# Residual projections by 512-column weight row tiles in one ring of eight PSUM banks, with regrouped stage seams

## The chip, the cores and the metric

The kernel runs on one core of a Trainium2 chip. The metric is the device time of one execution in microseconds, as the median of several runs. A core has a matrix engine (TensorE, PE in the profile), three engines for elementwise work (VectorE or DVE, ScalarE or ACT, GpSimd or POOL) and SyncE (SP), which here issues nearly all DMA transfers. Each engine has its own instruction list, which it works through in order; an instruction that waits for a semaphore holds up everything behind it on its engine. Matmuls read SBUF and accumulate in PSUM, which has eight banks of 128 partitions by 512 fp32 values.

## What is computed

One layer of a trunk block over 1024 tokens of width 1024, in fp32: a token mixer (RWKV-7 and HGRN2 branches, merged by gates), cross-attention into 256 memory tokens with four heads, and a SwiGLU feed-forward part, each with an RMSNorm before and a residual add behind, then a last RMSNorm.

```python
u = rmsnorm(h, norm_mix_g[l])
cols = u @ w_in[l]
...
h = h + (gate_a * y_a + gate_b * y_b) @ w_out[l]

u = rmsnorm(h, norm_xa_g[l])
m = rmsnorm(mem, norm_mem_g[l])
q = (u @ xa_wq[l]).reshape(B, S, XA_HEADS, XA_HEAD)
k = (m @ xa_wk[l]).reshape(B, n_mem, XA_HEADS, XA_HEAD)
v = (m @ xa_wv[l]).reshape(B, n_mem, XA_HEADS, XA_HEAD)
...
h = h + o @ xa_wo[l]

u = rmsnorm(h, norm_ffn_g[l])
h = h + (jax.nn.silu(u @ ffn_w1[l]) * (u @ ffn_w3[l])) @ ffn_w2[l]
...
return rmsnorm(h, norm_final_g)
```

The two products whose tiling changes are those by `w_out` and by `xa_wo`, each 1024 by 1024, each followed by a residual add.

## The kernel before

**Precision.** Every large product is done with split operands: a tile is copied by ACT into a rounded high part (`split`, L281), and POOL or DVE subtracts that from the tile for the low part (L285). A product of two split operands is three matmuls (`mm3`, L299 to L301: high by high, low by high, high by low). So each weight tile costs a DMA load, an ACT copy, a subtraction on POOL or DVE, and three matmuls per use. `P` is 128 rows, `HALF` 512 columns, `KT` 8 tiles of the contracted dimension, `NHALF` 2.

**The order.** The code is written in program order, and a scheduler builds each engine's list from it; parts in a `high_priority` block are pulled forward. Generators that are stepped by `next` inside a loop (`beside`, `late`) put other work into that loop's order.

**The stages.** Up to about 1299 us the mixer runs. `attention_block` follows: keys and values from the memory tokens (`pk`, `pvv`; `load_w` loads 256-column weight groups as four tiles of two row blocks, L1668), then the first residual projection, by `w_out`, then per half of the tokens and per head the queries (`pq`), scores (`psc`), softmax, transposes (`ptp`) and outputs (`po`), then the second residual projection, by `xa_wo`, for one half of the tokens after the other.

**The residual projections** (`add_project`, tile `pw`) go by four column groups of 256. For a group the four weight tiles are loaded and split; then for each pair of tokens tiles (128 tokens each) all eight `k` are run into one PSUM tile, and DVE adds it to the residual (L1758). A matmul has 256 columns. Between the pairs `beside` is stepped. For `w_out` and the first half of `xa_wo` that is `w2_sums`, which forms sums of blocks of `ffn_w2` for the last phase (loads `y` at L1713, a DVE and a POOL sum at L1717 and L1718, a store to `wsum_d` at L1721): seven of its eleven steps under `w_out`, four under `xa_wo`. Under the second half of `xa_wo` it is `early_blocks`, which prepares the FFN's operand blocks of the first half of the tokens.

**PSUM** in this stage is three pools: two banks for transposes, three for projections, three for scores and outputs.

**The FFN** forms its products by a Strassen-like scheme: sums of operand blocks, seven products (`P1` to `P7`) for each pair of row blocks. The products that need only the first half of the tokens are run first for `AHEAD` = 2 groups (`early_products`); the blocks of the second half (`late_blocks`: L1976 to L1981, operands `hB`, `lB`, `fS`, `hS`, `lS`) are made in two lumps ahead of and behind them.

**The last phase** multiplies by `ffn_w2`: seven blocks of eleven items. An item is a hidden tile (`tl`, loaded at L2194, split into `th` by ACT at L2200 and `tl` by DVE at L2201) and a weight tile (`wraw` from `ffn_w2` or `wsum_d`, L2176; split into `wh` by ACT and `wl` by POOL), and twelve matmuls of 512 columns into four accumulators `acc`. Loads run 8 items ahead, splits 4 ahead. At a block's end the accumulators are added into `hres`. After the fifth block, the first half of the tokens is complete: each token tile is scaled (`finish`, L2139 and L2143, DVE) and stored (L2142 and L2146, SP) at once. Then the second half follows, and the program ends.

Of the kernel before, what the change touches and what calls it, by code (L numbers as in the profile page):

```python
# [2 lines left out]

# [6 lines left out]
F32 = mybir.dt.float32  # L10
# [173 lines left out]
def tile_trunk(ctx, tc, x, mem, norm_mix_g, w_in, rw_mu, rw_w0, rw_w2, rw_a0, rw_a2, rw_g2,  # L184
# [1456 lines left out]
    ssq = const.tile([P, 4, 4], F32, name="ssq")  # L1641
# [5 lines left out]
    def attention_block(xctx):  # L1647
# [14 lines left out]
        def load_w(src, col, lo_eng=None, queue=nc.sync):  # L1662

            s3 = src[0, :, col:col + W].rearrange("(k p) c -> p k c", p=P)
            w = []
            for k in range(0, KT, 2):
                raw = rp.tile([P, 2, W], F32, tag="wraw", name="wraw")
                queue.dma_start(out=raw, in_=s3[:, k:k + 2, :])  # L1668
                hi, lo = (wp.tile([P, 2, W], F32R, tag=n, name=n) for n in ("whi", "wlo"))
# [10 lines left out]
        with tc.high_priority(4000):  # L1680
            w0 = load_w(xa_wv, 0, queue=nc.scalar)
# [3 lines left out]
        for c in range(D // W):  # L1685
            if 2 * c >= KEYS:
                w = load_w(xa_wk, c * W)
                for t in range(2):
                    ps = pp.tile([P, HALF], F32, tag="proj", name="pk")
# [6 lines left out]
            w = load_w(xa_wv, c * W) if c else w0  # L1696
            ps = pp.tile([P, NMT, W], F32, tag="proj", name="pvv")
# [9 lines left out]
        def w2_sums(fs, places):  # L1707
# [16 lines left out]
            for place in places:  # L1724
                if place:
                    y = place()
                    f = next(fs)
                    load(f, y)
                    loaded.append((f, y))
                    if len(loaded) < 3:  # L1730
                        yield
                        continue
                if loaded:
                    sums(*loaded.pop(0))
                yield
            for l in loaded:
                sums(*l)
                yield

        def add_project(a, w, src, halves, ss=None, beside=iter(()), every=False):  # L1740


            hs = []
            for c in range(D // W):
                ww = load_w(w, c * W)
                for i2 in range(2 * halves.start, 2 * halves.stop):
                    if c == 0:
                        hs += load_tokens(hp, src, 2 * i2, 2)
                    ps = pp.tile([P, 2, W], F32, tag="proj", name="pw")
                    for n in range(2):  # L1750
                        i = 2 * i2 + n
                        ah, al = a[i // 4]
                        ts_ = slice((i % 4) * P, (i % 4 + 1) * P)
                        for k in range(KT):
                            mm3(ps[:, n, :], ah[:, k, ts_], al[:, k, ts_], *ww[k], k == 0, k == KT - 1)
                    for n in range(2):
                        o = hs[2 * i2 + n - 4 * halves.start][:, c * W:(c + 1) * W]
                        nc.vector.tensor_tensor(o, ps[:, n, :], o, op=ALU.add)  # L1758
                        if ss is not None:
                            junk = sp.tile([P, D], mybir.dt.bfloat16, tag="junk", name="junkw", bufs=1)[:, 0:W]  # L1760
                            nc.scalar.activation(junk, o, AF.Square, accum_out=ss[:, 2 * i2 + n - 4 * halves.start, c:c + 1])
                    if every or c > 1 or c == 1 and i2 % 2:
                        next(beside, None)
            return hs

        def early_blocks(hs, hi, lo):

            sums = act2.tile([P, KT, HALF], F32, tag="ah", name="sums")
            for k in range(HK):
                pts = []  # L1770
                for kk in (k, k + HK):
                    pts.append(pt_.tile([P, HALF], F32, tag="tr", name="pt"))
                    for i in range(4):
                        nc.tensor.transpose(pts[-1][:, i * P:(i + 1) * P], hs[i][:, kk * P:(kk + 1) * P], ident)
                b12, s1 = sums[:, k, :], sums[:, k + HK, :]
# [8 lines left out]
                if k % 2:  # L1784
                    yield


        yT = []
        for h in range(NHALF):
            a = act((act0, act1)[h])  # L1790
# [4 lines left out]
            yT.append(a)  # L1795
# [4 lines left out]
        def in_act2(tag, n):  # L1800
# [6 lines left out]
        hs = add_project(yT, w_out, x[0], range(NHALF), every=True, beside=w2_sums(  # L1807
            w2f, [None, None] + [in_act2(tag, n) for tag in ("ah", "al", "ah") for n in range(2)] + [in_act2("al", 0)]))
        xaT = []
        for h in range(NHALF):  # L1810
            for i in range(4):
                nc.sync.dma_start(out=h1d[(4 * h + i) * P:(4 * h + i + 1) * P, :], in_=hs[4 * h + i])
            normalize(hs[4 * h:4 * h + 4], sp)
            a = act((act0, act1)[h])
            transpose_split(hs[4 * h:4 * h + 4], "xa", *a, slice(0, HALF), pt_)
            xaT.append(a)
# [4 lines left out]
        def weights(h, hd):  # L1821
# [4 lines left out]
            for t in range(2):  # L1826
                ps = pp.tile([P, HALF], F32, tag="proj", name="pq")
# [8 lines left out]
            for i2 in range(2):  # L1836
                ps = px.tile([P, 2, NM], F32, tag="x", name="psc")
# [17 lines left out]
        def attended(o, hd, p):  # L1855
            pTh = hp.tile([P, NMT, HALF], F32R, tag="h", name="pTh")
            pTl = hp.tile([P, NMT, HALF], F32R, tag="h", name="pTl")
            for mt in range(NMT):
                pt = pt_.tile([P, HALF], F32, tag="tr", name="ptp")
# [396 lines left out]
```

## Time and profile before

| | us |
|---|---|
| median of 3 runs (range) | 2383.24 (2382.25 to 2384.34) |
| the profiled execution | 2381.83 |
| its span | 2380.1 |
| mean granted TensorE clock | 0.990 of full |
| first and last `pw` matmul | 1357.6, 1709 |
| last phase, from and to | 2147, 2372 |

A row of the timeline gives a start and a duration in us, the engine, the line, and the operation as output <- inputs with its shape. In brackets stands how long the engine was idle before it, and what it waited for. A group row gives the number of instructions, their busy time and mean ns, and then the idle time before them. Matmuls are pipelined, so that the distance between their starts tells their cost, not their duration. The rows themselves stand in the prediction, beside the steps that use them.

### The profile page before, as it was taken

How to read it: one execution, taken by the hardware profiler on the slowest of the kernel's cores; microseconds unless marked ns; L12 is line 12 of the kernel's file. 1: busy time of each engine (PE TensorE's matmuls, PEld its weight loads, DVE VectorE, ACT ScalarE, POOL GpSimd, SP SyncE). 2: the span in 40 equal slices, each digit the busy share in tenths (PEclk: the TensorE clock that was granted, in tenths of full speed). 3: DMA queues.
4: the chain of work that ended last, by engine and by line, in shares of the span. 5: the costliest groups of instructions: out<-in, count | busy, mean ns of one | idle time of the engine just before them, and what ended most of it. 6: DMA issues, size and time to landing. Idle time of an engine off the chain costs nothing. (4 is left out here: it accounts for less than half of the span.)

```text
span 2380.1 us, 48890 instructions
## 1 busy us (share of the span) xinstructions
PE 2311.5 (97%) x19126; PEld 1913.0 (80%) x19126; DVE 1515.4 (64%) x2397; ACT 1136.1 (48%) x2271; POOL 1235.6 (52%) x1257
## 2 busy tenths in 40 slices
PE   7999999999999999999999999999989999999997
PEld 5777777778887878888887998889968888888876
DVE  5887874667777667766755545444577565566454
ACT  6545454545566646565564515442452333334432
POOL 3554545555566555675564741113465655556544
PEclk9999999999999999999999999999999999999999
DMA  5444445333334344434244893128643433348552
GB/s 176 116 126 119 124 119 166 70 95 85 103 102 121 78 130 107 114 90 115 64 150 142 272 339 128 63 70 305 201 136 100 128 100 100 111 151 319 181 173 93
DMA packets 397668, 325.97 MB, mean 137 GB/s; under 512 B 107467, under 2 KB 330813, under 8 KB 396029
## 3 DMA queue, kind: packets, MB, share of 16 engines
q1 hardware_dynamic: 395005, 317.08, 43.9%
q0 software_dynamic: 1344, 4.72, 0.5%
q8 instruction: 151, 2.47, 0.4%
q10 hardware_dynamic: 1088, 1.05, 0.1%
q14 instruction: 80, 0.66, 0.1%
HBM read 226.03 MB, written 96.21 MB: 135 GB/s over the span
## 5 line engine op out<-in xcount | busy, mean ns | idle before, releaser
L102 PE MATMUL pproj<-uh,whi 128*128 128x512 f32 x768 | 320.3, 417 | 0.9 <-DVE q L102 0.7
L102 PE MATMUL pproj<-uh,wlo 128*128 128x512 f32 x768 | 301.0, 392 | 3.2 <-POOL wlo L102 2.3
L102 PE MATMUL pproj<-ul,whi 128*128 128x512 f32 x768 | 301.4, 392 | 0.0
L285 POOL TENSOR_TENSOR wl<-wraw,wh 128x512 fp32r<-128x512 f32 x143 | 202.0, 1427 | 153.3 <-ACT wh L281 139.9
L285 POOL TENSOR_TENSOR wlo<-wraw,whi 128x512 fp32r<-128x512 f32 (+1 forms) x86 | 118.3, 1380 | 227.7 <-ACT whi L281 219.1
L281 ACT ACTIVATE whi<-wraw 128x512 fp32r<-128x512 f32 (+1 forms) x166 | 101.0, 617 | 188.4 <-DMA wraw<-in_w_out_dram 46.1
L102 POOL TENSOR_TENSOR wlo<-wraw,whi 128x512 fp32r<-128x512 f32 x96 | 128.5, 1349 | 119.3 <-ACT whi L102 106.2
L299 PE MATMUL pproj<-uh,whi 128*128 128x512 f32 (+1 forms) x432 | 179.7, 416 | 0.9 <-ACT whi L281 0.6
L301 PE MATMUL pproj<-uh,wlo 128*128 128x512 f32 (+1 forms) x432 | 170.9, 396 | 1.2 <-POOL wlo L285 1.2
L102 PEld LDWEIGHTS pproj<-uh,whi 128*128 128x128 f32 x768 | 144.4, 188 | 34.1 <-DVE q L102 2.0
L300 PE MATMUL pproj<-ul,whi 128*128 128x512 f32 (+1 forms) x432 | 170.7, 395 | 0.0
L102 PEld LDWEIGHTS pproj<-ul,whi 128*128 128x128 f32 x768 | 144.4, 188 | 32.4
L102 PEld LDWEIGHTS pproj<-uh,wlo 128*128 128x128 f32 x768 | 145.0, 189 | 28.8 <-POOL wlo L102 2.7
L300 PE MATMUL pw<-wlo,ah 128*128 128x256 f32 x512 | 146.7, 287 | 6.9 <-POOL wlo L285 4.6
L299 PE MATMUL pw<-whi,ah 128*128 128x256 f32 x512 | 146.1, 286 | 1.3 <-DVE tok L1758 1.3
L301 PE MATMUL pw<-whi,al 128*128 128x256 f32 x512 | 145.8, 285 | 0.0
L285 POOL TENSOR_TENSOR wlT<-wraw,whT 128x512 fp32r<-128x512 f32 x70 | 98.5, 1419 | 68.9 <-ACT whT L281 49.4
L299 PE MATMUL acc<-wh,th 128*128 128x512 f32 x308 | 121.5, 395 | 7.2 <-ACT wh L281 7.2
L2201 DVE TENSOR_TENSOR tl<-tl,th 128x512 fp32r<-128x512 f32 x77 | 77.1, 1028 | 79.1 <-ACT th L2200 75.2
L281 ACT ACTIVATE wh<-wraw 128x512 fp32r<-128x512 f32 x143 | 86.4, 622 | 82.5 <-PE P L300 57.3
L300 PE MATMUL acc<-wl,th 128*128 128x512 f32 x308 | 122.2, 397 | 2.0 <-POOL wl L285 2.0
L102 ACT ACT_TABLE_LOAD x90 | 115.5, 1283 | 13.5 <-DVE m L102 6.4
(456 smaller groups left out, 6551.9 us busy)
## 6 DMA issues: line engine op xcount, KB each, us to landing
wraw<-in_w_in_dram SPq DMA_DIRECT2D x148, 256.0 KB
wraw<-in_ffn_w_dram SPq DMA_DIRECT2D x137, 256.0 KB
y<-in_ffn_w_dram SPq DMA_DIRECT2D x22, 512.0 KB
wsum_d<-y SPq DMA_DIRECT2D x11, 1024.0 KB
hsum_d<-s SPq DMA_DIRECT2D x44, 256.0 KB
tl<-hsum_d SPq DMA_DIRECT2D x44, 256.0 KB
wraw<-wsum_d SPq DMA_DIRECT2D x44, 256.0 KB
hid_d<-s SPq DMA_DIRECT2D x33, 256.0 KB
```

The lines of the kernel that those rows point to most:

```text
L102: r = getattr(self.engine, op)(*a, **kw)
L281: nc.scalar.activation(hi, src, AF.Copy)
L285: e.tensor_tensor(lo, src, hi.bitcast(F32), op=ALU.subtract)
L299: nc.tensor.matmul(ps, ah, bh, start=first, stop=False)
L300: nc.tensor.matmul(ps, ah, bl, start=False, stop=False)
L301: nc.tensor.matmul(ps, al, bh, start=False, stop=last)
L2201: tt(hl, hl.bitcast(F32), hh.bitcast(F32), op=ALU.subtract)
```

## The change

1. *The residual projections* go by two column halves of 512. For a half, the eight weight tiles of one row block each (128 rows by 512 columns) are loaded and split one after the other; each meets all token tiles as it comes, so that all token tiles accumulate at once in eight PSUM banks (four for `xa_wo`, which runs a half of the tokens at a time). The last three `k` (`ILAST`) are run token by token, so that each token's accumulator is done before the next one's. A matmul has 512 columns.
2. *PSUM*: the three pools of the attention stage become one ring of eight banks.
3. *The seam into attention*: the first value weights are only loaded at high priority; their splits stand at their place in program order.
4. *`w2_sums`* gets a table of steps: eight of its eleven sums under `w_out`, three under the first half of `xa_wo`. The first half's normalization starts after its last `w_out` token (`between`), the transposes of the second half move into the attention loop, and finished tokens are stored one by one (`dst`).
5. *The FFN's start*: `AHEAD` is 3 instead of 2, the early weights come in another order, and one of the four late blocks is made after the sixth, eighth, tenth and twelfth early product.
6. *The last phase*: DVE takes the low part of two weight tiles in three, POOL the third. The finish of the first half's tokens goes into the list `later`, of which one or two entries are run per item.

```diff
-        pt_ = xctx.enter_context(tpool(name="xa_t", bufs=2, space=PSUM))
-        pp = xctx.enter_context(tpool(name="xa_p", bufs=3, space=PSUM))
-        px = xctx.enter_context(tpool(name="xa_x", bufs=3, space=PSUM))
+        pp = xctx.enter_context(tpool(name="xa_p", bufs=8, space=PSUM))
...
-            w0 = load_w(xa_wv, 0, queue=nc.scalar)
+            w0 = list(load_raw(xa_wv, 0, nc.scalar))
...
-            for c in range(D // W):
-                ww = load_w(w, c * W)
...
+            for c in range(NHALF):
+                cs = slice(c * HALF, (c + 1) * HALF)
+                ps = {i: pp.tile([P, HALF], F32, tag="p", name="pw") for i in tiles}
+                ww = []
+                for k in range(KT):
+                    raw = rp.tile([P, HALF], F32, tag="wraw", name="wraw")
+                    nc.sync.dma_start(out=raw, in_=w[0, k * P:(k + 1) * P, cs])
+                    hi, lo = (wp.tile([P, HALF], F32R, tag=n, name=n) for n in ("whi", "wlo"))
+                    split(hi, lo, raw, lo_eng=("pool", "dve")[k % 2])
+                    ww.append((hi, lo))
...
+                    if k < KT - ILAST:
+                        for i in tiles:
+                            step(a, ps, ww, i, k)
+                    if k < KT - 1:
                         next(beside, None)
+                for n, i in enumerate(tiles):
+                    for g in range(KT - ILAST, KT):
+                        step(a, ps, ww, i, g)
+                    o = hs[n][:, cs]
+                    nc.vector.tensor_tensor(o, ps[i], o, op=ALU.add)
...
+        hs = add_project(yT, w_out, x[0], range(NHALF), between=normed, beside=w2_sums(
+            w2f, [([in_act2(loads[g], n) for n in range(2)] if g in loads else [],
+                   int(g in (7, 8, 9, 10, 11, 12, 14, 15))) for g in range(16)]))
...
-    AHEAD = 2
...
     for f in range(AHEAD):
-        early_products(f, *early[f])
-    next(late)
+        for _ in early_products(f, *early[f]):
+            n += 1
+            if n == 5:
+                early.append(early_operands(weights(2, True)))
+            if n > 5 and n % 2 == 0:
+                next(late)
...
+            later.extend((lambda: nc.vector.tensor_scalar(o1, o1, r, None, op0=ALU.mult), last,
+                          lambda: (store(1 - c, o1), store(c, o2))))
...
-        ops[b, f] = (hh, hl, *operand(y, "2"))
+        ops[b, f] = (hh, hl, *operand(y, "2", "pool" if f % 3 == 2 else "dve"))
...
-        if later:
-            more(*later.pop(0))
+        for _ in range(2 if len(later) > HF else 1):
+            if later:
+                later.pop(0)()
```

Line numbers move by one to some forty lines: L281 becomes L282, L285 L286, L1668 L1665 or, for the weight tiles of the residual projections, L1754.

The first place is ACT at the seam from the mixer to attention, first before, then with the change; `sa` is the mixer's gate from the key half `pproj`, and `whi` the high part of the first value weights.

```order
L102 ACTIVATE sa<-pproj 128x512
L102 ACTIVATE junkh,sth<-poh 128x128 x4
L1668 DMA wraw<-in_xa_wv_dram 128x2x256 x4
L281 ACTIVATE whi<-wraw 128x512 x3
L102 ACTIVATE sa<-pproj 128x512
L281 ACTIVATE whi<-wraw 128x512 x5
```

```order
L103 ACTIVATE sa<-pproj 128x512
L103 ACTIVATE junkh,sth<-poh 128x128 x4
L1665 DMA wraw<-in_xa_wv_dram 128x2x256 x4
L103 ACTIVATE sa<-pproj 128x512
L282 ACTIVATE whi<-wraw 128x512 x8
```

The second `sa` stood behind three of the splits and now stands ahead of all eight.

The second place is SP from the end of the first half of `xa_wo` on, first before, then with the change; `h_d<-tok` stores a finished token tile, `wraw<-in_xa_wo` loads a weight tile of the second half, `wraw<-in_ffn_w` one of the FFN, and `early_d<-sums` stores FFN operand blocks.

```order
L1668 DMA wraw<-in_xa_wo_dram 128x2x256 x3
L1897 DMA h_d<-tok 128x1024 x2
L1668 DMA wraw<-in_xa_wo_dram 128x2x256 x3
L1897 DMA h_d<-tok 128x1024 x2
L1668 DMA wraw<-in_xa_wo_dram 128x2x256 x6
L1782 DMA early_d<-sums 128x512 x2
L1783 DMA early_d<-sums 128x512 x2
L1782 DMA early_d<-sums 128x512
L1783 DMA early_d<-sums 128x512
L1782 DMA early_d<-sums 128x512
L1783 DMA early_d<-sums 128x512
L1924 DMA wraw<-in_ffn_w_dram 128x4x128 x16
```

```order
L1754 DMA wraw<-in_xa_wo_dram 128x512 x3
L1774 DMA h_d<-tok 128x1024
L1754 DMA wraw<-in_xa_wo_dram 128x512
L1774 DMA h_d<-tok 128x1024 x2
L1941 DMA wraw<-in_ffn_w_dram 128x4x128 x16
L1774 DMA h_d<-tok 128x1024
L1754 DMA wraw<-in_xa_wo_dram 128x512 x5
L1796 DMA early_d<-sums 128x512
```

The sixteen FFN loads stood behind all of the projection's weight tiles; now they stand ahead of the last nine, the first of which is the eighth tile of the first column half.

The third place is SP in the last phase, where the first half's tokens are stored (`out_dram<-hres`), first before, then with the change; `tl<-hid_d` and `wraw<-wsum_d` load the hidden and the weight tile of an item to come.

```order
L2176 DMA wraw<-wsum_d 128x512
L2142 DMA out_dram<-hres 128x512
L2146 DMA out_dram<-hres 128x512
L2194 DMA tl<-hid_d 128x512
L2142 DMA out_dram<-hres 128x512
L2146 DMA out_dram<-hres 128x512
L2176 DMA wraw<-wsum_d 128x512
L2142 DMA out_dram<-hres 128x512
L2146 DMA out_dram<-hres 128x512
L2142 DMA out_dram<-hres 128x512
L2146 DMA out_dram<-hres 128x512
L2176 DMA wraw<-wsum_d 128x512 x3
```

```order
L2217 DMA wraw<-wsum_d 128x512
L2172 DMA out_dram<-hres 128x512 x2
L2235 DMA tl<-hid_d 128x512
L2172 DMA out_dram<-hres 128x512 x2
L2217 DMA wraw<-wsum_d 128x512 x2
L2172 DMA out_dram<-hres 128x512 x2
L2217 DMA wraw<-wsum_d 128x512 x2
L2235 DMA tl<-hid_d 128x512
L2217 DMA wraw<-wsum_d 128x512
L2172 DMA out_dram<-hres 128x512 x2
```

The eight stores stood within ten rows with one load of a hidden tile between them; now the last pair stands behind the next such load.

More of the change, by code (lines that the diff above doesn't have):

```diff
@@ L2 @@
 from contextlib import ExitStack
+from itertools import chain
 import concourse.bass as bass
@@ L1723, in w2_sums @@
             loaded = []
[L1724 to L1727, printed above, removed]
+            for loads, summed in steps:
+                for place in loads:
+                    y, f = place(), next(fs)
                     load(f, y)
                     loaded.append((f, y))
[L1730 to L1733, printed above, removed]
+                for _ in range(summed):
@@ L1764, in add_project @@
             return hs
         def early_blocks(hs, hi, lo):
-            sums = act2.tile([P, KT, HALF], F32, tag="ah", name="sums")
+            b12s, s1s = (vp.tile([P, HK, HALF], F32, tag=t, name="sums") for t in ("Vh", "Vl"))
             for k in range(HK):
@@ L1805, in in_act2, with normed @@
             return place
[L1807 to L1810, printed above, removed]
+        loads = {4: "ah", 5: "al", 9: "ah", 11: "al"}
+        def normed(hs):
             for i in range(4):
[L1812 to L1816, printed above, removed]
+                nc.sync.dma_start(out=h1d[i * P:(i + 1) * P, :], in_=hs[i])
+            normalize(hs[0:4], sp)
+        hs = add_project(yT, w_out, x[0], range(NHALF), between=normed, beside=w2_sums(
+            w2f, [([in_act2(loads[g], n) for n in range(2)] if g in loads else [],
+                   int(g in (7, 8, 9, 10, 11, 12, 14, 15))) for g in range(16)]))
+        xaT = [act(pool) for pool in (act0, act1)]
+        transpose_split(hs[0:4], "xa", *xaT[0], slice(0, HALF), pp, tag="p")
+        for i in range(4, 8):
+            nc.sync.dma_start(out=h1d[i * P:(i + 1) * P, :], in_=hs[i])
+        normalize(hs[4:8], sp)
         oT = []
@@ L2018, in tile_trunk, with weights @@
     tt = nc.vector.tensor_tensor
-    def weights(f):
-        return [[raw(w, k, (f + e) * P, HK, P) for e in (0, HF) for k in (0, HK)] for w in WS]
+    AHEAD = 3
+    def weights(f, early=False):
+        if not early:
+            return [[raw(w, k, (f + e) * P, HK, P) for e in (0, HF) for k in (0, HK)] for w in WS]
+        A = [{}, {}]
+        for b in (0, 2, 3, 1):
+            for n, w in enumerate(WS):
+                A[n][b] = raw(w, b % 2 * HK, (f + b // 2 * HF) * P, HK, P)
+        return [[a[b] for b in range(4)] for a in A]
     def early_operands(A):
@@ L2084, in products @@
             s = gated(n, U2[n], s, f + HF, 1)
-    AHEAD = 2
     with tc.high_priority(600):
-        early = [weights(f) for f in range(AHEAD)]
+        early = [weights(f, True) for f in range(2)]
         early = [early_operands(A) for A in early]
```

137 lines of the change are left out of this document (70 added, 67 removed).

## The prediction

> **What bounds the kernel now.** I read the page's busy shares first, then the table of stretches for PE, then the timeline of each stretch in which PE stands idle.
>
> ```profile
> span 2380.1 us, 48890 instructions
> PE 2311.5 (97%) x19126; PEld 1913.0 (80%) x19126; DVE 1515.4 (64%) x2397; ACT 1136.1 (48%) x2271; POOL 1235.6 (52%) x1257
> 1299.00:1320.00 21.00, 15.05 (x104) 0.84 0.71 239
> 1375.00:1400.00 25.00, 21.66 (x166) 0.93 0.97 366
> 1400.00:1420.00 20.00, 18.74 (x156) 1.00 0.91 328
> 1420.00:1457.00 37.00, 37.00 (x311) 1.00 0.56 191
> 1457.00:1466.00 9.00, 7.07 (x42) 1.00 0.71 233
> 1630.00:1650.00 20.00, 16.51 (x119) 0.83 0.86 305
> 1680.00:1709.00 29.00, 28.66 (x240) 1.00 0.59 187
> 1736.00:1764.00 28.00, 21.19 (x74) 0.88 0.26 76
> 2147.00:2290.00 143.00, 143.00 (x631) 1.00 0.68 238
> 2290.00:2345.00 55.00, 45.78 (x177) 0.91 0.47 157
> ```
>
> The columns of the stretches are its bounds and length, PE's busy time (and matmuls), the granted clock, the DMA share and GB/s. TensorE is the bound: 97% busy, and from 2147 to 2290 it never waits. So a change pays either by giving PE less to do or by closing one of the stretches where it waits. What a stretch loses is its idle time plus length times (1 − clock): 21 − 15.05 + 21 × 0.16 = 9.3 us at 1299 to 1320, 5.1 and 1.3 in the two from 1375, 1.9 at 1457, 6.9 at 1630 (a little too much: part of the slow clock fell into idle time), 0.3 at 1680, 10.2 at 1736, 14.2 at 2290. Together some 49 us, nearly all the waiting after 1299. Before 1299 the two programs issue the same instructions in the same order, so nothing changes there.
>
> **The change part by part.** *The matmuls of the projections.*
>
> ```profile
> L299 PE MATMUL pw<-whi,ah x512: 276/283/420, 1357.6 to 1709.1; 128*128 128x256 f32 x171
> 1379.79 0.28 PE L299 MATMUL pw<-whi,ah 128*128 128x256 f32 x1
> ...
> 1381.22 0.28 PE L299 MATMUL pw<-whi,ah 128*128 128x256 f32 x1
> 1383.59 0.39 PE L300 MATMUL pw<-wlo,ah 128*128 128x256 f32 x1 [2.08 <-POOL wlo L285]
> 2284.61 0.39 PE L300 MATMUL acc<-wl,th 128*128 128x512 f32 x1
> ...
> 2286.20 0.39 PE L301 MATMUL acc<-wh,tl 128*128 128x512 f32 x1
> ```
>
> Durations overlap, so I count from start to start: 1379.79 to 1381.22 is 12 steps, 0.119 us for 256 columns; 2284.61 to 2286.20 is 7 steps, 0.227 for 512. There are three lines of 512, 1536 matmuls × 0.119 = 183 us; 768 of 512 columns × 0.227 = 174. **−9**. The adds and splits that go with them move the same elements.
>
> [...]
>
> *The seam into attention (1299 to 1320).*
>
> ```profile
> 1308.41 0.63 ACT L281 ACTIVATE whi<-wraw 128x512 fp32r<-128x512 f32 x1 [0.89 <-DMA wraw<-in_xa_wv_dram]
> 1308.95 0.58 ACT L102 ACTIVATE sa<-pproj 128x512 f32<-128x512 f32 x1
> 1304.31 0.39 PE L299 MATMUL pvv<-whi,mT 128*128 128x256 f32 x1 [1.93 <-ACT whi L281]
> 1305.65 0.39 PE L300 MATMUL pvv<-wlo,mT 128*128 128x256 f32 x1 [0.95 <-POOL wlo L285]
> 1309.58 5.21 PE L102 MATMUL pproj<-mT,wkey 128*128 128x256 f32 x24 [3.07 <-ACT sa L102]
> ```
>
> ACT holds `sa` behind three splits that wait for DMA (the last of them is shown), and PE waits 3.07 us for it. In the new order `sa` comes ahead of them. What is late next are the splits for `pvv`, whose loads land as before (1.93 + 0.95), now behind 5 us of key matmuls. The 3.07 go, and 1 us of slow clock with them: **−4** (−2 to −6).
>
> *w_out (1357 to 1457).* Before, PE waits for `wlo` of the second column group. Now a group needs eight tiles instead of four, and its last three together, after 5 × 8 × 3 matmuls × 0.227 = 27.2 us. On SP the loads of the sixth to eighth stand behind eight token loads and up to eight `y` loads; the splits stand behind the sums on POOL and DVE.
>
> ```profile
> L285 POOL TENSOR_TENSOR wlo<-wraw,whi 128x512 fp32r<-128x512 f32 x10 | 14.3, 1441 | 25.2 <-ACT whi L281 25.0
> L285 DVE TENSOR_TENSOR wlo<-wraw,whi 128x512 fp32r<-128x512 f32 x10 | 11.6, 1176 | 13.1 <-ACT whi L281 13.1
> L1718 POOL TENSOR_TENSOR y<-y 128x512 f32<-128x512 f32 x7 | 9.5, 1358 | 24.3 <-DVE y L1717 14.7 <-DMA y<-in_ffn_w_dram 9.6
> ```
>
> From 1357 on, eight token tiles and eight `y` tiles of 512 KB are 8.4 MB, at 328 to 366 GB/s 23 to 26 us; with what is queued ahead the tile behind them lands at about 27 to 30 us, and three sums of 1.36 us plus a split of 1.44 on POOL bring its low part to 33 or 35: a wait of 6 to 8 us, against 6.4 lost before. **+1** (−4 if the prefetched weights come first, +6 if the sums pile up).
>
> *The query seam* (1.9 us): the second half's 32 transposes move into the attention loop and the first normalization under the last four tokens, each 2.04 us of matmuls. In exchange they come in one block, with splits of 0.63 us behind. **0** (−2 to +2).
>
> *xa_wo, first half (1630).* The loss of 6.9 us came from `wlo` of weight tiles that were loaded late behind the sums. Now the eight tiles of the first column group are issued before the sums' loads. **−4.5** (−2 to −5).
>
> *xa_wo, second half.* Only 0.3 us was lost at 1680 to 1709. Now SP issues 16 FFN weight loads ahead of the last token's store and of the eighth weight tile, which is needed after 5 × 4 × 3 × 0.227 + 6 × 0.227 = 15.0 us. Those loads are 4.2 MB, at the 305 GB/s of 1630 to 1650 13.8 us. With issue and landing the eighth tile is there at about 16, its ACT split is behind seven of 0.63 us for the FFN (20.5), its low part behind DVE's FFN differences (1.57 us below) at 22 to 23. A wait of 7, and a cold stretch after it: **+8** (0 if the tile slips ahead, +14 if two tiles are late).
>
> [...] The trace shows shorter ones paid for too: the wait of 2.08 us at 1383 was followed by a clock of 0.93 over 25 us, that is 3.5 us at half rate (25 × 0.07 × 2). [...]
>
> *The FFN's start.*
>
> ```profile
> 1742.63 0.79 PE L300 MATMUL P<-lB,wh 128*128 128x512 f32 x1 [3.06 <-DVE lB L1977]
> 1762.95 0.50 PE L300 MATMUL P<-lS,whT 128*128 128x512 f32 x1 [2.66 <-DVE lS L285]
> L2059 DVE TENSOR_TENSOR wraw<-wraw 128x512 f32<-128x512 f32 x3 | 4.7, 1567 | 0.0
> ```
>
> Before, the late operand blocks are made in a lump between early products, and PE waits for `lB`, then for `lS`. Now there are 12 early products instead of 8 (12 × 12 × 0.227 = 32.7 us of PE), and one of four blocks is made behind every second one, so each has 5.4 us; DVE's part of a block is some six operations of 0.7, 4.4 us. What is left is about 2 us of 10.2. **−8** (−5 to −9). No products are added in all: those of the third group leave the main loop.
>
> *The last phase (2147 to 2372).*
>
> ```profile
> L285 POOL TENSOR_TENSOR wl<-wraw,wh 128x512 fp32r<-128x512 f32 x72 | 102.4, 1437 | 75.1 <-ACT wh L281 64.1 <-DMA wraw<-in_ffn_w_dram 8.7 <-DMA wraw<-wsum_d 2.2
> L2201 DVE TENSOR_TENSOR tl<-tl,th 128x512 fp32r<-128x512 f32 x67 | 66.0, 1013 | 75.0 <-ACT th L2200 71.1 <-PE acc L301 3.9
> SPq L2176 <- POOL wl L285: 70.0, 34, 5.1
> 2311.94 0.38 SPq L2194 DMA_DIRECT2D tl<-hid_d  x1
> 2322.50 0.33 SPq L2146 DMA_DIRECT2D out_dram<-hres  x1
> 2325.45 0.38 SPq L2194 DMA_DIRECT2D tl<-hid_d  x1
> 2330.90 0.63 ACT L2200 ACTIVATE th<-tl 128x512 fp32r<-128x512 f32 x1 [12.72 <-DMA tl<-hid_d]
> 2332.10 0.80 PE L299 MATMUL acc<-wh,th 128*128 128x512 f32 x1 [5.91 <-ACT wh L281]
> ```
>
> Two things run out here. SP waits 70 us for POOL's `wl`, 1.44 us each, to free the buffer of the next weight load; the `tl` load queues behind. And SP stands in the stores of the first half until 2322.50, so that the next `tl` load goes out at 2325.45, lands at 2330.90, and PE waits 5.91. After the change DVE takes two of three `wl` (1.18 us as above), a circle of two items shortens by about 0.5 us, and the first half's finish is dealt out one or two steps an item, with one pair of stores at a time between the loads; one `tl` load still stands behind three pairs. Of 14.2 us I leave 4: **−10** (−13 to +5, if DVE is late for a whole block).
>
> Sum: −9 − 4 + 1 + 0 − 4.5 + 8 − 8 − 10 = **−26.5**. The profiled execution took 2381.8 us, 1.7 around its span; that gives 2355.3. The median of the runs, 2383.2, is 1.4 above the profiled one: **2356.7**.
>
> **The rivals.**
> - *w_out is paced by loads.* From 1375 to 1420 the DMA share is 0.91 to 0.97, and eight sums instead of seven are put there, 2 MB more or 6 us at 350 GB/s. Then w_out's half of the saving (4.5 us) vanishes and 6 us are waited for: 2367.2. Against it: 0.56 in the 37 us behind, room for the added 2 MB.
> - *The late tiles cost double* (the eighth tile of xa_wo's second half 14 us, w_out +6): 2356.7 + 6 + 5 = 2367.7, with one more half-rate stretch of 3.4 us (1.7 lost) 2369.4. For it: every cost of waiting here has come with a slow clock. Against it: a DMA share of only 0.59 before 1709.
> - *All seams close*: w_out −4, second half of xa_wo 0, last phase −13: 2356.7 − 5 − 8 − 3 = 2340.7.
> - *Slower: DVE becomes what the last phase waits for.* An item gives PE 12 × 0.227 = 2.72 us. DVE would have 1.01 + ⅔ × 1.18 = 1.8 an item, 20 for a block of 11; where block sums (8 × 1.2, as `wlo`), PSUM adds (8 × 0.7) and a finish (4 × two operations of about 1.0, as `tl`) fall into the same block, 43 against PE's 30. If the operands ahead do not cover it and two blocks each lose 13, the −10 turns into +26: 2392.7. It decides where DVE's work stays above 2.72 us an item for longer than the four items of lead. Against it: over the whole phase DVE would be busy some 160 of 225 us.
> - *The change does not do what it says*: the pitch with eight accumulators in turn is no better than two of 256 columns (0.238). Then the 9 us stay: 2365.7. [...] Against it, from the rows: `acc` above also goes through four accumulators, at 0.227.
>
> **How the numbers follow.** The forecast 0.55; all seams 0.13; loads 0.11; double tiles 0.13; pitch 0.04; DVE 0.04. The range, 2340 to 2372, leaves out the slower case, half of the doubled tiles' worst end and a little at the low end, about 0.15. The kernel's measurement tells 0.2%, 4.8 us, from no change: faster (below 2378.5) 0.93, same 0.04, slower 0.03.
>
> **What would show it.** After: 768 `pw` matmuls 0.227 apart; no wait of PE for `sa`; PE waits of 5 to 9 us for the sixth to eighth tile of w_out's first group, and for the eighth tile in xa_wo's second half, with a granted clock near 0.8 there; about 2 us of idle time at the FFN's first products; no wait above 3 us behind the first half's stores. The forecast is wrong if DVE, not PE, is above 90% busy in the last three blocks, if the DMA share of w_out stays at 0.95 to its end, or if the two late tiles cost more than 16 us together.

## The result, and the profile after

The changed kernel takes 2345.27 us in the median of 4 runs (2344.14 to 2346.70), beside 2383.79 for the kernel before in the same series: a ratio of 0.9838 with a 95% interval of 0.9821 to 0.9856, or 38.5 us faster. Forecast were 2356.7 with a range of 2340 to 2372, so the time lies in the range and the gain was put 12 us too low. By its number the rival "all seams close" (2340.7) is nearer than the forecast, but w_out and the second half of `xa_wo`, which it closes, stayed open. The profiled execution has a span of 2343.8, 36.3 less than before.

These are the head of the page and the same table of stretches for PE, at the places to which they have moved (bounds and length, PE busy and its matmuls, granted clock, DMA share, GB/s):

```profile
span 2343.8 us, 47246 instructions
PE 2290.4 (98%) x18358; PEld 1869.2 (80%) x18358; DVE 1536.7 (66%) x2425; ACT 1135.2 (48%) x2259; POOL 1154.6 (49%) x1201
1299.00:1320.00 21.00, 17.43 (x123) 0.92 0.91 310
1375.00:1400.00 25.00, 20.52 (x76) 0.86 0.99 373
1453.00:1462.00 9.00, 9.00 (x56) 1.00 0.55 188
1470.00:1485.00 15.00, 13.74 (x79) 1.00 0.14 45
1620.00:1645.00 25.00, 25.00 (x109) 1.00 0.84 298
1645.00:1690.00 45.00, 39.12 (x180) 0.92 1.00 302
1720.00:1760.00 40.00, 40.00 (x189) 1.00 0.25 73
2110.00:2255.00 145.00, 145.00 (x640) 1.00 0.70 241
2255.00:2310.00 55.00, 55.00 (x245) 1.00 0.56 181
```

The FFN's start (1720 to 1760) and the whole last phase have no idle time left, nor has the first half of `xa_wo` (1620 to 1645). PE still waits 3.6 us at the seam into attention and 1.3 us at the query seam. The two larger stretches that are left are w_out at 1375 to 1400 and the second half of `xa_wo` at 1645 to 1690. By the measure of the prediction (idle time plus length times one minus the clock), before and after:

| stretch | before | forecast for after | after |
|---|---|---|---|
| seam into attention | 9.3 | 5.3 | 5.3 |
| w_out | 6.4 | 7.4 | 8.0 |
| query seam | 1.9 | 1.9 | 1.3 |
| xa_wo, first half | 6.9 (too high) | 2.4 | 0 |
| xa_wo, second half | 0.3 | 8.3 | 9.5 (too high) |
| FFN's start | 10.2 | 2.2 | 0 |
| last phase | 14.2 | 4.2 | 0 |

The rows marked "too high" count some slow clock that fell into idle time. Counted from start to start of the matmuls, against their usual distance in the same half, the losses are 6.7 before in the first half and 8.0 after in the second.

A second account goes by the lengths of the stages, each from its first matmul to that of the next. The forecast is the prediction's, with the −9 for the matmuls put on the four halves of the projections in equal parts:

| stage | before | after | difference | forecast |
|---|---|---|---|---|
| up to the first key matmul (`pproj<-mT`) | 1299.3 | 1300.1 | +0.8 | 0 |
| seam, keys and values, to the first `pw` | 58.3 | 55.3 | −3.0 | −4 |
| w_out (to its last `pw`) | 99.5 | 96.8 | −2.7 | −3.5 |
| heads, to the first `pw` of `xa_wo` | 147.1 | 144.6 | −2.4 | 0 |
| `xa_wo`, first half | 54.8 | 48.7 | −6.1 | −6.75 |
| `xa_wo`, second half (to its last `pw`) | 50.4 | 54.9 | +4.5 | +5.75 |
| FFN, to the first `acc` | 438.2 | 426.2 | −12.0 | −8 |
| last phase, to the last `acc` | 224.6 | 209.2 | −15.4 | −10 |

The 8.0 us behind the last `acc` are the same in both.

These are PE, ACT and POOL around the wait in w_out (start, duration, operation; in brackets the idle time before it and its cause):

```profile
1386.24 0.49 PE L300 MATMUL pw<-whi,ah 128*128 128x512 f32 x1 [0.93 <-ACT whi L282]
1389.64 0.75 PE L301 MATMUL pw<-wlo,ah 128*128 128x512 f32 x1 [2.90 <-POOL wlo L286]
1385.56 1.24 ACT L282 ACTIVATE whi<-wraw 128x512 fp32r<-128x512 f32 x2 [9.45 <-DMA wraw<-in_w_out_dram]
1387.10 1.26 POOL L1722 TENSOR_TENSOR y<-y 128x512 f32<-128x512 f32 x1
1388.32 1.26 POOL L286 TENSOR_TENSOR wlo<-wraw,whi 128x512 fp32r<-128x512 f32 x1
```

ACT has stood idle for 9.45 us until the late tiles landed, and POOL makes the low part only behind a sum of `y`. That is the wait that was forecast, among the tiles and on the engines that were forecast. PE stands idle for 0.93, 2.90 and 0.64 us around it, 4.5 in all, and the slow clock costs another 3.5.

These are SP, DVE, ACT and PE in the second half of `xa_wo`:

```profile
1644.72 16.22 SPq L1941 DMA_DIRECT2D wraw<-in_ffn_w_dram  x16
1660.98 0.83 SPq L1774 DMA_DIRECT2D h_d<-tok  x1
1661.86 2.96 SPq L1754 DMA_DIRECT2D wraw<-in_xa_wo_dram  x5
1668.23 0.74 DVE L314 TENSOR_SCALAR tok<-tok,ss 128x1024 f32<-128x1024 f32 x1
1668.28 0.61 ACT L282 ACTIVATE whi<-wraw 128x512 fp32r<-128x512 f32 x1
1669.03 1.12 PE L1788 MATMUL pt<-ident,tok 128*128 128x128 f32 x4 [5.88 <-DVE tok L314]
```

The 16 FFN loads hold SP for 16 us. Behind them come the store of the last token and the eighth weight tile. PE's wait of 5.88 us has the name of the last token's normalization, which overwrites the tile in place and so has to follow its store. The eighth tile's high part is made at the same moment, 1668.28. Which of the two held PE, the row alone cannot say.

These are DVE's groups and SP's waits for the low parts in the last phase:

```profile
L2242 DVE TENSOR_TENSOR tl<-tl,th 128x512 fp32r<-128x512 f32 x70 | 52.7, 768 | 57.9 <-ACT th L2241 57.4
L286 DVE TENSOR_TENSOR wl<-wraw,wh 128x512 fp32r<-128x512 f32 x56 | 43.0, 772 | 3.1 <-ACT wh L282 2.9
SPq L2217 <- DVE wl L286: 41.7, 23, 4.9
SPq L2217 <- POOL wl L286: 12.6, 7, 3.4
```

`tl` takes 768 ns in the mean instead of 1013 on the same engine, and a low part 772 ns on DVE instead of 1437 on POOL. POOL keeps 21 of the 77 low parts, three items in a block of eleven. SP's waits for them fall from 70 to 54 us.

### The profile page after: what moved, and what is told of

The parts are those of the page before. It is cut to its first block, busy times and chain, and to the rows that moved or that the text cites. A ratio compares the mean times of both kernels' runs of the same rounds, so it can differ in the third digit from the quotient of the medians.

```text
span 2343.8 us, 47246 instructions
## 1 busy us (share of the span) xinstructions
PE 2290.4 (98%) x18358; PEld 1869.2 (80%) x18358; DVE 1536.7 (66%) x2425; ACT 1135.2 (48%) x2259; POOL 1154.6 (49%) x1201
## 5 line engine op out<-in xcount | busy, mean ns | idle before, releaser
L286 POOL TENSOR_TENSOR wl<-wraw,wh 128x512 fp32r<-128x512 f32 x87 | 121.5, 1404 | 201.5 <-ACT wh L282 159.0
L286 POOL TENSOR_TENSOR wlo<-wraw,whi 128x512 fp32r<-128x512 f32 (+1 forms) x86 | 114.3, 1330 | 215.2 <-ACT whi L282 212.7
L282 ACT ACTIVATE whi<-wraw 128x512 fp32r<-128x512 f32 (+1 forms) x166 | 100.9, 618 | 183.1 <-DMA wraw<-in_w_out_dram 61.4
L286 POOL TENSOR_TENSOR wlT<-wraw,whT 128x512 fp32r<-128x512 f32 x72 | 101.5, 1420 | 70.3 <-ACT whT L282 58.9
L282 ACT ACTIVATE wh<-wraw 128x512 fp32r<-128x512 f32 x143 | 87.3, 624 | 96.6 <-PE P L301 72.5
L103 ACT ACT_TABLE_LOAD x90 | 115.5, 1283 | 14.2 <-DVE m L103 7.2
L302 PE MATMUL acc<-wh,tl 128*128 128x512 f32 x308 | 119.8, 389 | 0.0
L301 PE MATMUL pw<-wlo,ah 128*128 128x512 f32 x256 | 102.0, 399 | 3.7 <-POOL wlo L286 2.9
L286 DVE TENSOR_TENSOR wlo<-wraw,whi 128x512 fp32r<-128x512 f32 x80 | 69.2, 868 | 53.4 <-ACT whi L282 53.2
L300 PE MATMUL pw<-whi,ah 128*128 128x512 f32 x256 | 102.2, 400 | 0.9 <-ACT whi L282 0.9
```

The lines of the kernel that those rows point to most:

```text
L103: r = getattr(self.engine, op)(*a, **kw)
L282: nc.scalar.activation(hi, src, AF.Copy)
L286: e.tensor_tensor(lo, src, hi.bitcast(F32), op=ALU.subtract)
L300: nc.tensor.matmul(ps, ah, bh, start=first, stop=False)
L301: nc.tensor.matmul(ps, ah, bl, start=False, stop=False)
L302: nc.tensor.matmul(ps, al, bh, start=False, stop=last)
```

## The experiments

Each kernel is the changed one with the edit shown, unless said otherwise. Times are medians; the ratios are to the kernel before, run on the same chip beside it, with the 95% interval. Since a step of 3 us is smaller than an interval, the verdicts rest on the profiles, and the ratios are held beside them. A profile is one execution. How far one can be trusted is told by the traces here in which a stage's own code was left as in the changed kernel: w_out takes 94.3 to 96.8 us in them, the second half of `xa_wo` 53.6 to 55.8, the FFN 425.9 to 426.0 from its first product to the first `acc`, and the last phase 209.2 to 209.6, but 212.8 in one.

### The width of the matmul

```diff
-            mm3(ps[i], ah[:, k, ts_], al[:, k, ts_], *ww[k], k == 0, k == KT - 1)
+            for e in range(2):
+                es = slice(e * 256, (e + 1) * 256)
+                mm3(ps[i][:, es], ah[:, k, ts_], al[:, k, ts_], *(t[:, es] for t in ww[k]),
+                    k == 0 and e == 0, k == KT - 1 and e == 1)
```

> The changed kernel with every projection matmul cut into two of 256 columns: same weight tiles, same loads, same order of the steps, 1536 matmuls in place of 768. Theory (the pitch in the rows of before, 0.119 against 0.227 us): 9 us slower than the changed kernel, about 2354, all of it spread evenly over the projection steps. [...] Second rival (the new loop lost nothing because its loads set the pace): no change within 1 us and longer PE waits gone in exchange.

Measured: 2353.22, ratio 0.9875 (0.9859 to 0.9892), against 0.9838 for the changed kernel: some 9 us slower, span 2353.3. But the number agrees for a mixed reason: the wait before the second half's transposes grew from 5.88 to 11.50 us. So the same cut was made once more in the kernel in which the waits are gone (the last one below).

> The kernel with later sums and a priority of 100 (PE waits in the projections almost gone), with every projection matmul cut into two of 256 columns. Without the long wait behind xa_wo's first half, which grew by 5.6 us when the same cut was made in the changed kernel, this is the price of the narrower matmul alone. Theory (0.120 us for 256 columns throughout): the projections take 10 us more, the span is about 2341. Rival (the narrow matmul costs 0.1135 us in part of the kernel, as in the first half of xa_wo of the earlier run): 4 to 7 us more, 2335 to 2338.

Measured: 2341.53, ratio 0.9828 (0.9814 to 0.9841), against 0.9805 without the cut: 5.5 us slower, span 8.3 longer. These are PE's stretches without idle time, first two with 512, then two with 256 columns, and then two places in the first half of `xa_wo`, 6 steps of 512 and 12 of 256 apart:

```profile
1400.00:1420.00 20.00, 20.00 (x90) 1.00 0.91 342
1605.00:1625.00 20.00, 20.00 (x87) 1.00 0.70 262
1400.00:1420.00 20.00, 20.00 (x169) 1.00 0.95 360
1605.00:1625.00 20.00, 20.00 (x179) 1.00 0.81 296
1619.74 0.39 PE L301 MATMUL pw<-wlo,ah 128*128 128x512 f32 x1
...
1621.14 0.39 PE L301 MATMUL pw<-wlo,ah 128*128 128x512 f32 x1
1619.74 0.28 PE L300 MATMUL pw<-whi,ah 128*128 128x256 f32 x1
...
1621.10 0.28 PE L300 MATMUL pw<-whi,ah 128*128 128x256 f32 x1
```

The counts include two or three matmuls that overlap a border, so the distance from start to start is the better measure. In w_out two narrow matmuls take 2 × 0.120 = 0.240 us where a wide one takes 0.227. In the first half of `xa_wo` it is 2 × 1.36/12 = 0.227 against 1.40/6 = 0.233: there the narrow ones are the faster. Summed over all `pw` matmuls from start to start the narrow form takes 185.4 us and the wide one 178.2. These sums still hold some slow and late steps; with the usual distances alone (0.120 for narrow and 0.227 for wide, but 0.1135 and 0.233 in the first half of `xa_wo`) they are 181.8 and 175.4. The width alone is worth 6.4 us, not 9, and the first half of `xa_wo` loses 1.2 by it. So the rival expectation was right in its cause, and by the medians in its 4 to 7 us; of the 8.3 us by which the span is longer, some 2 are waits and slow clock.

### The late tiles of xa_wo's second half

```diff
-    with tc.high_priority(600):
+    with tc.high_priority(300):
```

> The changed kernel with the priority of the FFN's early weights lowered from 600 to 300. On SP the last token's store of xa_wo's first half now stands ahead of 15 of the 16 FFN loads, the eighth weight tile of the second half still behind them. PE's wait of 5.88 us at 1669 is named as one for the normalized last token (its operation writes in place and so waits for that store). Theory A (only the store is to blame): the wait goes, 7 to 8 us faster, about 2338. Theory B (the forecast: the eighth tile and its splits are as late): PE waits 3 to 5 us some microseconds later, for wlo, and only 2 to 4 us are gained, about 2342.

Measured: 2346.33, ratio 0.9849 (0.9835 to 0.9864). There is no gain. These are ACT and PE in it, and the stretch:

```profile
1666.70 1.13 ACT L282 ACTIVATE whi<-wraw 128x512 fp32r<-128x512 f32 x2
1667.36 1.22 PE L300 MATMUL pw<-whi,ah 128*128 128x512 f32 x2 [6.33 <-ACT whi L282]
1645.00:1690.00 45.00, 38.67 (x175) 0.92 0.97 281
```

The transposes run on time now, and PE waits 6.33 us for the eighth tile instead. Theory A falls. Theory B has the cause right, though its 2 to 4 us of gain did not come either: the tile was fully as late as the token.

The same with a priority of 200:

> The same with priority 200: the last token's store and the eighth weight tile both stand ahead of all 16 FFN loads. Theories A and B both: the whole loss of 8 us goes, about 2337. If this is no faster than priority 300, A is right; if it is 4 us faster, B is. Rival: the FFN's weights are now late at its first products, and up to 8 us are given back there.

Measured: 2342.48, ratio 0.9834 (0.9819 to 0.9848). PE and the stretch:

```profile
1668.88 0.50 PE L300 MATMUL pw<-whi,ah 128*128 128x512 f32 x1 [2.42 <-ACT whi L282]
1671.39 0.79 PE L301 MATMUL pw<-wlo,ah 128*128 128x512 f32 x1 [2.01 <-POOL wlo L286]
1645.00:1690.00 45.00, 40.56 (x184) 0.92 1.00 292
```

The eighth tile is in time, and the next tile, the first of the second column half, is late: 4.4 us of idle time and the same slow clock. The second half takes 54.2 us, within the scatter of the unchanged code. Both expectations of a full gain failed. What stood behind the 16 loads on SP was late each time: PE's wait had the name of the last token (5.88 us), then of the eighth tile (6.33), then of the first tile of the second column half (2.42 and 2.01).

### The sums under w_out

```diff
-        loads = {4: "ah", 5: "al", 9: "ah", 11: "al"}
+        loads = {7: "ah", 8: "al", 11: "ah", 13: "al"}
...
-                   int(g in (7, 8, 9, 10, 11, 12, 14, 15))) for g in range(16)]))
+                   {9: 1, 10: 1, 11: 1, 12: 1, 13: 1, 14: 1, 15: 2}.get(g, 0)) for g in range(16)]))
```

> The changed kernel with the loads of the ffn_w2 blocks under w_out moved from the steps 4, 5, 9, 11 to 7, 8, 11, 13, and their sums to 9 to 15, so that all eight weight tiles of the first column half are issued ahead of them. Theory (the wait of 2.90 us for wlo and the cold stretch at 1384 to 1392, 8 us in all, come from loads and sums that stand ahead of the tiles): 6 to 8 us faster, about 2338. Rival (the DMA is full there, share 0.99, and the sums' loads and POOL work only move the wait into the second column half or to the queries): less than 3 us faster, with a PE wait after 1400.

Measured: 2338.27, ratio 0.9814 (0.9800 to 0.9829), span 2335.9, 7.9 below the changed kernel's. The stretch of the wait:

```profile
1375.00:1400.00 25.00, 25.00 (x112) 1.00 1.00 384
```

There is no idle time and no slow clock, at a DMA share of 1.00 and with the same eight sums. The wait came from what stood ahead of the tiles, not from a full DMA, and it did not come back further on: w_out takes 88.9 us, and the stages behind it are as long as in the changed kernel.

### The last phase

Low parts on POOL:

```diff
-        ops[b, f] = (hh, hl, *operand(y, "2", "pool" if f % 3 == 2 else "dve"))
+        ops[b, f] = (hh, hl, *operand(y, "2", "pool"))
```

> The changed kernel with the low parts of all weight tiles of the last phase on POOL again; the first half's finish stays dealt out over the items. Theory A (the circle of POOL's wl, SP's weight load and the tl load behind it ran out of lead before): PE waits again in the last blocks, 3 to 8 us in all, 4 to 9 us slower than the changed kernel. Theory B (the stores of the first half in one lump were the whole loss): within 1.5 us of the changed kernel, SP's waits for POOL come back to about 70 us and cost nothing.

Finish at once:

```diff
         if h == 0:
-
-            later.extend((lambda: nc.vector.tensor_scalar(o1, o1, r, None, op0=ALU.mult), last,
-                          lambda: (store(1 - c, o1), store(c, o2))))
-            return
-        nc.scalar.activation(o1, o1, AF.Copy, scale=r)
+            nc.vector.tensor_scalar(o1, o1, r, None, op0=ALU.mult)
+        else:
+            nc.scalar.activation(o1, o1, AF.Copy, scale=r)
...
-            if h == 0:
-                finish(h, i, c, None)
-                return
             if i:
                 finish(h, i - 1, c, sums[h, i])
...
-        for _ in range(2 if len(later) > HF else 1):
+        for _ in range(1):
```

> The changed kernel with the first half's tokens scaled and stored at once at the end of the fifth block, as before; DVE keeps two of three low parts. Theory A: with the shorter circle there is lead enough to cover the lump, 0 to 3 us slower. Theory B: the lump alone brings back 6 us of waiting near the sixth block and a stretch of slow clock, 7 to 10 us slower. If DVE is what the last phase then waits for (scaling, adds and low parts in one block), 10 us or more slower.

Both:

> Both undone together: low parts on POOL, finish at once. It should give back the whole last phase of before: PE waits of about 9 us and 5 us lost to the slow clock between the fourth block and the sixth, 13 to 16 us slower than the changed kernel. If the two parts are independent this is the sum of the two kernels above; if either alone suffices it is far more than the sum.

Measured: 2347.22, 2345.64 and 2353.61; ratios 0.9860 (0.9838 to 0.9882), 0.9848 (0.9830 to 0.9865) and 0.9873 (0.9852 to 0.9893). These are PE from 2270 to 2315 in the three, the longest wait in the first and the row that carries the third. Behind them stand the same stretch and its longest wait in the kernel with two groups of early products (below), which leaves the last phase as it is:

```profile
2270.00:2315.00 45.00, 42.66 (x179) 0.96 0.49 158
2270.00:2315.00 45.00, 44.51 (x195) 1.00 0.46 156
2270.00:2315.00 45.00, 39.01 (x156) 0.92 0.49 165
2285.68 0.50 PE L301 MATMUL acc<-wl,th 128*128 128x512 f32 x1 [1.04 <-POOL wl L286]
2303.68 0.80 PE L300 MATMUL acc<-wh,th 128*128 128x512 f32 x1 [4.40 <-ACT wh L282]
2270.00:2315.00 45.00, 42.73 (x186) 1.00 0.52 173
2289.27 0.50 PE L301 MATMUL acc<-wl,th 128*128 128x512 f32 x1 [1.59 <-DVE wl L286]
```

Lost are 2.34 + 45 × 0.04 = 4.1 us, 0.5 us and 6.0 + 3.6 = 9.6 us; by the length of the whole phase it is 5.1, 1.1 and 10.1. Theory A fits both single edits: the shorter circle seems the larger part, and with it the lump of stores is nearly free. But the kernel with two groups of early products lost 2.3 us of idle time here, 3.6 by the length of the phase, without any change to it, so the first number is not clear of what a single profile can show. Together the two edits cost more than the sum of both; each covers some of the other. It is less than the 13 to 16 expected, and of the 14.2 us lost before (15.4 by the length) some 5 stay unassigned.

The first of these kernels also tests DVE's faster subtraction. Its only edit is that POOL makes all low parts, and with it the same subtraction for `tl`, 768 ns in the changed kernel, is back near the 1013 of before:

```profile
L2242 DVE TENSOR_TENSOR tl<-tl,th 128x512 fp32r<-128x512 f32 x67 | 65.7, 1005 | 72.7 <-ACT th L2241 71.3 <-PE acc L300 1.3
```

### The FFN's start

The blocks in one lump:

```diff
-            if n > 5 and n % 2 == 0:
-                next(late)
+    for _ in range(4):
+        next(late)
```

> The changed kernel with the four late blocks of the FFN made in one lump behind the twelfth early product, instead of one after the 6th, 8th, 10th and 12th; three groups of early products as in the change. Theory A (spreading the blocks beneath the products is what closed the stretch): 5 to 10 us slower, with PE waits for lB and lS behind the early products. Theory B (the third group of early products gives the weights and the second half's tokens time enough): within 2 us.

Two groups of early products, blocks spread:

```diff
-    AHEAD = 3
+    AHEAD = 2
...
-            if n == 5:
-                early.append(early_operands(weights(2, True)))
-            if n > 5 and n % 2 == 0:
+            if n > 4:
                 next(late)
```

> The changed kernel with two groups of early products in place of three, the late blocks made after the 5th to 8th product. With spreading alone (4 products, 10.9 us of PE, over four blocks of about 4.4 us of DVE each) the blocks come later than the products end: 3 to 6 us slower than the changed kernel, waits before the first late products. If spreading alone suffices and the third group is idle luxury: within 1 us.

Measured: 2350.22, ratio 0.9868 (0.9850 to 0.9886), and 2347.61, ratio 0.9849 (0.9834 to 0.9864). PE from 1720 to 1760 in the first, with its longest wait, and in the second:

```profile
1720.00:1760.00 40.00, 34.74 (x162) 1.00 0.16 46
1755.92 0.50 PE L301 MATMUL P<-lS,whT 128*128 128x512 f32 x1 [2.66 <-DVE lS L286]
1720.00:1760.00 40.00, 38.99 (x177) 1.00 0.26 77
```

The lump costs 5.3 us of idle time (7.2 by the length of the FFN), with the wait for `lS` of before at its old length. Two groups with spread blocks lose 1.0 us here (1.5 by the length of the FFN). So spreading closes most of the stretch, and the third group saves about a microsecond more. The expectation of 3 to 6 us was too high. Of the FFN's 12.0 us the two edits bring back 8.7; the rest is not assigned. The span of 2346.4 also holds the 2.3 us of idle time in the last phase that were shown above and that the changed kernel does not have; why is open.

### The seam into attention

```diff
-            w0 = list(load_raw(xa_wv, 0, nc.scalar))
+            w0 = load_w(xa_wv, 0, raws=load_raw(xa_wv, 0, nc.scalar))
...
-            w = load_w(xa_wv, c * W, raws=None if c else w0)
+            w = load_w(xa_wv, c * W) if c else w0
```

> The changed kernel with the splits of the first value weights at high priority again, so that the gate copy sa stands behind three of them on ACT. Theory: PE's wait of 3 us for sa comes back, 2 to 4 us slower than the changed kernel. Rival: the wait only changes its name, since what is behind (the value weights' splits) is late by the same DMA: within 1 us.

Measured: 2346.02, ratio 0.9846 (0.9829 to 0.9862), span 2348.8. PE's wait and the stretch:

```profile
1311.07 5.41 PE L103 MATMUL pproj<-mT,wkey 128*128 128x256 f32 x24 [7.12 <-ACT sa L103]
1299.00:1320.00 21.00, 13.55 (x91) 0.76 0.72 236
```

The wait for `sa` comes back, longer than the 3.07 us of before, and the stretch loses 7.5 + 5.0 = 12.5 us against 5.3. In the profile the theory holds, with 7 us rather than 2 to 4. The new order puts the key matmuls ahead of `pvv`, so PE has nothing else to do while it waits for `sa`. In the medians no difference can be told: the profiled execution, 2350.46, is the slowest of four, and the other three took 2344.26 to 2346.68. That `sa` can hold PE in this order is shown; what it costs in most executions is not.

### A version that beats both

The later sums and a priority of 100 for the FFN's early weights:

> The changed kernel with the ffn_w2 sums later, as in the run that moved them, and the priority of the FFN's early weights lowered to 100, by which the eighth weight tile and the first four of the second column half of xa_wo's second half stand on SP ahead of the FFN loads. If the priority of 200 gained only 2 us because the next tile in line (the first of the second column half) came behind the 16 loads, the wait at 1655 now goes: 8 us less than with the sums moved alone, about 2331. Rival (the 16 loads of 4.2 MB have to come through before the FFN anyway, and PE waits for them at its first products): 2335 to 2338, with a wait near 1700.

Measured: 2335.39 in 5 runs, ratio 0.9805 (0.9789 to 0.9822); span 2331.1. The stretch of the late tiles, and the FFN's first products:

```profile
1640.00:1680.00 40.00, 37.82 (x183) 1.00 0.96 288
1720.00:1760.00 40.00, 39.26 (x177) 1.00 0.33 96
```

2.2 us of waiting are left of nine, and 0.7 at the FFN's first products: the loads are needed later than they were issued. The FFN takes 1.1 us longer for it, the second half of `xa_wo` 5.3 less than in the changed kernel. The span is 12.7 below the changed kernel's, 4.8 below that with the sums moved alone. In the medians the gain over the changed kernel is about 8 us (0.9838 against 0.9805). The time of 2331 that was expected was met by the profiled span, not by the median, which lies at the rival's 2335; the wait near 1700 that the rival names is not there beyond the 0.7 us.

## Why the prediction was right

**The bound.** That PE is the bound and that a change pays by less work or by closing a stretch was right: PE is busy 98% of the span after the change, and what each stage gave stands in the table of stage lengths, whose differences add up to the 36.3 us. Four of the seven stages came within 1.3 us of the forecast; the heads, the FFN and the last phase gave 2.4, 4.0 and 5.4 more. That the median is in the range is in part luck: several terms were mis-sized, and the matmuls' error stands against the others.

**The matmuls.** The 768 `pw` matmuls are there, 0.227 us apart in the median. The forecast −9 was too much: it took one place in w_out as the price of all. Before, too, the narrow matmuls of the first half of `xa_wo` were 0.1135 apart, and after the change the wide ones there are 0.233 apart. With these the term is 181.8 to 175.4, −6.4, the same as in the cut kernel. The rival by which the pitch gives nothing falls, though it holds for that one quarter.

**The seam**, −4: measured −4.0 in the stretch, −3.0 by the stage. PE's wait for `sa` is gone, and it came back in the profile of the kernel that put the splits back.

**w_out**, +1: measured +1.6, with the tile and the POOL sum named. The sum was met with other parts: it had a wait of 6 to 8 us and no slow clock, and the wait was 4.5 with 3.5 of slow clock. That the two gave the same is luck, and w_out takes 94.3 to 96.8 us in traces with the same code, so that its difference from the forecast is within the scatter. The rival in which loads pace this stage had a full DMA for it (share 0.99), but the share fell to 0.65 between 1400 and 1420, and the kernel with later sums ran the same stretch at a share of 1.00 without a wait. The order on SP and POOL was the cause, not the transfer rate. The forecast's own sign against it, more than 16 us for the two late tiles together, was just reached: from start to start the late steps of w_out and of `xa_wo`'s second half lost about 8 us each, and the forecast itself had 7.4 and 8.3 there.

**The query seam**, 0: the loss of 1.9 went, and a wait of 1.3 us came up before the `ptp` transposes at 1480. The heads as a whole took 2.4 us less; what the rest of that comes from is open.

**xa_wo**, −4.5 and +8: the 6.7 us of waiting and slow clock in the first half are gone, and the dearer wide matmuls there take 1.2 back; no run tests the cause by itself. In the second half the loss rose from 0.3 to 8.0 us. This was the boldest term, and its cause was tested: loads for the FFN ahead of the eighth tile. The row of the profile names the last token's normalization instead, which the forecast had seen only as a store; both were behind the same 16 loads and equally late.

**The FFN's start**, −8, and **the last phase**, −10: measured −10.2 and −14.2. By the lengths of the stages it is −12.0 and −15.4. Here the forecast was short, by more than 9 of the span's 10 us. Both times I left a residue (2 and 4 us) where nothing remained. For the last phase the residue was put on one `tl` load behind three pairs of stores, and PE has no idle time there. What was also mis-sized is DVE's price: I took 1.18 us for a low part and 1.01 for `tl` from rows in which POOL had all or half of the low parts; where POOL had 21 of the 77 they took 0.77. It goes with how the low parts are dealt out: in the kernel in which only that is undone, `tl` is back at 1.005. By what it comes no run shows. The lower price is also why the slower rival, with DVE as the bound, was far from coming true: the subtractions took 70 × 0.768 + 56 × 0.772 = 97 us, and DVE was busy 128 of 209 us between the first and the last `acc`, not the 160 of 225 that the rival counted.

**The slow clock**: in the trace of before, the waits of 2.08 us (to 1383.59) and 1.25 us (to 1385.82) were followed by a granted clock of 0.50 from 1386.0 to 1389.4. These 3.4 us at half rate, 1.7 lost, are the stretch that the rival of the doubled tiles adds. After the change, the waits in w_out, 0.93 and 2.90 us with one matmul between them, were followed by 0.50 from 1390 to 1396 (0.86 over the 25 us), and waits of 0.57 and 1.04 in the last phase with POOL's low parts by 0.96 over 45. But the lump in the FFN's start waited 2.66 us and smaller bits at a clock of 1.00, and so did waits of 0.53 and 1.59 at the same place of the last phase in the kernel with two groups. In these traces the length of a wait does not tell whether it will cost more than itself. Nor did every wait of before come with a slow clock, as the prediction has it for that rival: the stretches from 1400 and from 1457 have 1.26 and 1.93 us of idle time at 1.00.

**What stays open.** It is open why 256 columns cost 0.120 us in w_out and 0.1135 in the first half of `xa_wo` of one and the same kernel, while 512 columns cost more in the second place than in the first. Open are also some 5 us of the last phase and 3 of the FFN, which none of the edits brought back.

## What to carry to other kernels

In a kernel in which one engine is busy 97% of the time, list each stretch in which it still waits, and ask of the change what stands ahead of the late tile in each queue: this gave four of seven stages to within 1.3 us. Read the price of an instruction in every stage that uses it: one place in w_out stood for all and made the matmuls' term 2.6 us too large. Ask of a block of loads pulled forward by priority what falls behind it: here 16 loads made the store late as well as the next weight tile, and taking one of the victims out showed the next (waits of 5.88, 6.33 and 4.4 us). And read a duration again where a plan moves work between two engines: DVE's subtraction for `tl` took 1.013 us where POOL made all low parts, and 0.768 where it made 21 of 77.

## What the runs showed of the hardware

DVE's subtraction for `tl`, 128 by 512 fp32 values, took 1013 ns in the mean in the last phase of before, where POOL made all 77 low parts, 768 in the changed kernel, where POOL made 21 of them, and 1005 where only that was undone. Matmuls had two prices within one execution: those of 256 columns 0.120 us in w_out and 1.36/12 = 0.113 in the first half of `xa_wo` (the cut kernel), those of 512 columns 0.227 and 1.40/6 = 0.233 (the kernel without the cut). The granted clock stood at 0.50 for 3.4 us behind waits of 2.08 and 1.25 us in w_out of before, and at 1.00 over the 40 us that hold a wait of 2.66 us in the kernel with the late blocks in one lump.
